# The first three neighbourhood score units, computed in front of the second half of the query projections

## The chip, the cores and the metric

The kernel runs on one core of a Trainium2 chip. The metric is device time in microseconds (us) for one execution, 783.11 us as the median of three runs (781.49 to 783.5). The core has five engines, each with an instruction list of its own: TensorE (PE) multiplies matrices and writes PSUM, VectorE (DVE), ScalarE (ACT) and GpSimd (POOL) work on tiles in SBUF and (the first two) in PSUM, and SyncE (SP) issues the loads. They wait for one another by semaphores.

## The reference, cut to what matters

Two transformer blocks over 256 tokens with 1024 features. The change lies in the attention of the first, which has two mixers side by side: a latent attention (MLA, 8 heads) and a neighbourhood attention (8 heads of 64), whose outputs are joined. Of the second, per head, for the 256 queries in 4 rows of 64 columns:

```
s     = einsum('bqhd,bjkhd->bhqjk', qr, kr) * scale + bias       # own window: all 4 rows, 16 columns near the query
s     = where(col_in, s, MASK_VALUE).reshape(B, H, GRID_W, kh * GRID_W)
s_ctx = einsum('bqhd,bchd->bhqc', qr, k_ctx) * scale             # 256 tokens of context
p     = softmax(concatenate([s, s_ctx], axis=-1))
out   = p_win @ vr + p_ctx @ v_ctx
```

The queries are `hx @ w_in[:, 384:896]`, where `hx` is the normalized and modulated input. After the attention come an output projection, a mixture of 16 experts, and the second block.

## The kernel before, in words

Everything is one function, `build`, which writes out each engine's work. PE's list is kept as written (`MANUAL`); the lists of DVE, ACT and SP are made by a scheduler from the same program, by its own estimate of when things are ready. PE runs float32 in parts: a tile is split into a high part (a cast on ACT, L314) and a low part (a subtraction on DVE, L315), and three matmuls (L334 to L336) multiply high by high, low by high and high by low.

Projections stage. `proj` (eight steps of three matmuls) makes 128 columns at a time. The neighbourhood queries have 512 columns: two weight loads (`c` is 0 or 1), each of two tiles (`j`) of two heads. For each head the result is copied twice, scaled, into both halves of `NQH` (ACT, L647), and the low parts go to `NQL` (DVE, L648); these copies and subtractions of one head take turns. So `c = 0` makes heads 0 to 3, `c = 1` heads 4 to 7. Between them, and after, stand matmuls of the modulation (`mod_step`, L396).

Attention stage. A unit is one block of 128 queries of one head (`Unit`): head 0, 1, 2, ... of the first block, then of the second. `scores` multiplies `NQH` and `NQL` by the head's 512 keys into one PSUM bank (L683, L684), adds the bias in two pieces (DVE, L690) and calls `softmax`: the maximum (DVE, L664), the exponential and its sum (ACT, L667), the reciprocal (DVE, L668), the scaling (DVE, L669). `turn` transposes the result (L698, copied by ACT, L700), and `values` multiplies two units by the values (L710). `attend` runs `scores` three units (`LEAD`) ahead of `turn`, and puts other work, the `fills`, between: first the MLA queries (`uq`: two products, each with weights of its own in two pieces of 768 and 384 columns, tile `qHL`), then the MLA keys and values. `P` is the ring of four buffers that hold the softmax results, `big` a pool of 13 larger tiles, `bank()` a ring of 8 PSUM banks. SP loads weights into a ring of four `raw` buffers, each load waiting until the buffer is free.

Of the kernel before, what the change touches and what calls it, by code (L numbers as in the profile page):

```python
# [10 lines left out]
F32 = mybir.dt.float32  # L11
F32R = mybir.dt.float32r
I32 = mybir.dt.int32
AF = mybir.ActivationFunctionType
OP = mybir.AluOpType
AX = mybir.AxisListType
PSUM = bass.MemoryType.PSUM

P = 128
D = 1024  # L20
KD = 8
T = 256
# [79 lines left out]
LEAD = 3  # L102
# [109 lines left out]
def build(tc, xT, cT, consts, constsA, constsZ, vec, wmod, wA, relb, wE, wC, sgw, sgb, sgln, gfin, out, dbg=None):  # L212
    nc = tc.nc
    vat = VEC_AT
    cat, catA, catZ = [c.at for c in _consts()]
    mm = nc.tensor.matmul
# [6 lines left out]
    with ExitStack() as top:  # L223
# [31 lines left out]
        def vv(name):  # L255
            a, b = vat[name]
            return V[:, a:b]

        def cst(name):
            a, b = cat[name]  # L260
            return C[:, a:b]

        ident = cst("ident")
        cnt = [0]

        def nm_(base):
            cnt[0] += 1
            return f"{base}{cnt[0]}"

        def bank():  # L270
            return psp.tile([P, 512], F32, name=nm_("b"), tag="b")
# [4 lines left out]
        after = [None]  # L276
# [14 lines left out]
        def load(src, n=2048, pl=None, cuts=1):  # L291
            t = (pl or rawp).tile([P, 2048], F32, name=nm_("raw"), tag="raw")
            for a, b in pieces(n, cuts):
                queue(nc.sync.dma_start(t[:, a:b], src[:, a:b]))
            return t

        splitpools = [wp]
        turn = [0]

        def split(src, n=2048, pl=None):  # L300
            return halves(load(src, n, pl), n)
# [27 lines left out]
        def pairhl(name):  # L329
            return (ho.tile([P, KD, T], F32R, name=name + "H", tag="tH"), ho.tile([P, KD, T], F32R, name=name + "L", tag="tL"))  # L330
# [34 lines left out]
        with ExitStack() as sa:  # L365
# [3 lines left out]
            def bigt(shape, name, dt=F32):  # L369
                n = int(np.prod(shape[1:]))  # L370
                t = big.tile([P, 2048], dt, name=name, tag="raw")
                t = t[:shape[0], :n]
                if len(shape) == 3:
                    return t.rearrange("p (a b) -> p a b", a=shape[1])
                if len(shape) == 4:
                    return t.rearrange("p (a b c) -> p a b c", a=shape[1], b=shape[2])
                return t
# [20 lines left out]
            def mod_step(i):  # L398
                due.append((i, load(wmod[8 + i])))
                while len(due) > 1:  # L400
                    mod_mm(*due.pop(0))
# [8 lines left out]
            def mod_cols(hf, rows):  # L410
                pt = bank()
                for i in range(4):
# [3 lines left out]
                nc.vector.tensor_add(mod2[:, o:o + 16].rearrange("p (j i) -> p j i", i=4), src,  # L416
                                     vv("b_mod")[:, 16 + o:32 + o].rearrange("p (j i) -> p j i", i=4))

            oH, oL = pairhl("o")
            with ExitStack() as sp:  # L420
                pp = pool(sp, "pp")
# [129 lines left out]
                class Latent:  # L551
                    def __init__(self, m, n, g, dim, tag, H, L):
                        self.m, self.n, self.g, self.dim, self.tag, self.H, self.L = m, n, g, dim, tag, H, L
                        self.lat = pp.tile([P, m, n], F32, name=f"lat{tag}", tag={"kv": "latkv", "q": "rows3"}[tag])
                        self.sl = pp.tile([P, n], F32, name=f"sl{tag}", tag={"kv": "slkv", "q": "slq"}[tag])
# [18 lines left out]
                NQH = bigt([P, 8, T], "NQH", F32R)  # L574
                NK = [bigt([P, 4, 512], f"NK{i}", F32R) for i in range(2)]
                NQL = bigt([P, 8, T], "NQL", F32R)
# [9 lines left out]
                for c, g in enumerate("BC"):  # L586
                    for j, (hl, ps) in enumerate(early[g]):
                        for hh in range(2):
                            h = 2 * (2 * c + j) + hh
                            own, other = slice(64 * hh, 64 * hh + 64), slice(64 - 64 * hh, 128 - 64 * hh)  # L590
                            k_ = NK[h // 4][:, h % 4]
# [11 lines left out]
                ps = proj(ch[1], 0, 512, 64)  # L603
# [9 lines left out]
                bias = []  # L613
                for i, bt in enumerate((bigt([P, 2048], "bias"), bigt([P, 1024], "biasL"))):
                    n = (32, 16)[i]
# [8 lines left out]
                for c in range(4):  # L624
# [5 lines left out]
                    h, l = ch[c % 2]  # L630
                    for kk in range(2):
                        k = 2 * c + kk
                        s = slice(kk * 512, (kk + 1) * 512)
                        for b in range(4):
                            tb = slice(b * P, (b + 1) * P)
                            mm3(pv[b], (hH[k][:, tb], hL[k][:, tb]), (h[:, s], l[:, s]), k == 0, k == KD - 1)
                for b in range(4):
                    nc.scalar.copy(NV[:, b], pv[b])
                for c in range(2):
                    for j, hl in enumerate(split(wA[5 + c])):  # L640
                        ps = proj(hl, 0, T)
                        for hh in range(2):
                            rw = slice(64 * hh, 64 * hh + 64)
                            other = slice(64 - 64 * hh, 128 - 64 * hh)
                            h = 2 * (2 * c + j) + hh
                            for to in (rw, other):
                                nc.scalar.activation(NQH[to, h], ps[rw, :T], AF.Copy, scale=0.125)  # L647
                                nc.vector.scalar_tensor_tensor(NQL[to, h], ps[rw, :T], 0.125, NQH[rw, h], op0=OP.mult, op1=OP.subtract)  # L648
                    mod_step(5 + c)
                    for i in range(7, NA_FROM if c else 7):  # L650
                        mod_step(i)

            ar = pool(sa, "ar", bufs=2)
            KM = [bigt([96, 4, 512], f"KM{i}") for i in range(2)]
            VM = bigt([P, 4, 512], "VM")
            QM = bigt([96, 8, T], "QM")
            for km in KM:
                nc.vector.tensor_copy(km[64:96], kr[0:32].unsqueeze(1).to_broadcast([32, 4, 512]))

            lexp = [None]  # L660

            def softmax(ps, n):
                nm = ar.tile([P, 1], F32, name=nm_("nm"), tag="nm", bufs=3)
                nc.vector.tensor_reduce(nm, ps, axis=AX.X, op=OP.max, negate=True)  # L664
                rs = ar.tile([P, 1], F32, name=nm_("rs"), tag="rs", bufs=3)
                pt = ar.tile([P, 512], F32, name=nm_("P"), tag="P", bufs=LEAD + 1)
                lexp[0] = nc.scalar.activation(pt[:, :n], ps, AF.Exp, bias=nm, accum_out=rs)  # L667
                nc.vector.reciprocal(rs, rs)  # L668
                after[0] = nc.vector.tensor_scalar(pt[:, :n], pt[:, :n], rs, None, op0=OP.mult)  # L669
                return pt  # L670

            class Unit:
                def __init__(self, pair, na, b, hh, group):
                    self.pair, self.na, self.b, self.hh, self.group = pair, na, b, hh, group

                def scores(self):
                    pair, b, hh = self.pair, self.b, self.hh
                    h = 2 * pair + hh
                    tb = slice(b * P, (b + 1) * P)
                    ps = bank()  # L680
                    if self.na:
                        k_ = NK[h // 4][:, h % 4]
                        mm(ps, NQH[:, h, tb], k_, start=True, stop=False)  # L683
                        mm(ps, NQL[:, h, tb], k_, start=False, stop=True)  # L684
                        pw = ps[:, :T].rearrange("p (r c) -> p r c", r=4)
                        if b:
                            nc.vector.tensor_add(pw, pw, bias[0][:, :, h])
                        else:
                            for i in range(2):
                                nc.vector.tensor_add(pw[:, 2 * i:2 * i + 2], pw[:, 2 * i:2 * i + 2], bias[i][:, 2 - 2 * i:4 - 2 * i, h])  # L690
                    else:
                        mm(ps, QM[:, h, tb], KM[h // 4][:, h % 4], start=True, stop=True)
                    self.p = softmax(ps, 512)

                def turn(self):
                    pt = bank()
                    for kb in range(4):
                        nc.tensor.transpose(pt[:, kb * P:(kb + 1) * P], self.p[:, kb * P:(kb + 1) * P], ident)  # L698
                    self.pS = ar.tile([P, 512], F32, name=nm_("pS"), tag="pS", bufs=4)
                    nc.scalar.copy(self.pS, pt)  # L700

            def values(ua, ub):
                pair, b, na = ua.pair, ua.b, ua.na
                tb = slice(b * P, (b + 1) * P)
# [8 lines left out]
                nc.vector.tensor_sub(oL[:, c, tb], po[:, :P], oH[:, c, tb])  # L713

            def attend(na, fills, every, extra):
                us = [Unit(pair, na, b, hh, None) for b in range(2) for pair in range(4) for hh in range(2)]
                fills = list(fills)
                n = len(us)
                done = 0
                for i in range(LEAD):  # L720
                    us[i].scores()
                for i, u in enumerate(us):
                    if i + LEAD < n:
                        us[i + LEAD].scores()
                    want = -(-len(fills) * (i + 1) // n)
                    while done < want:
                        fills[done]()
                        done += 1
                    u.turn()
                    if i == n - 1:  # L730
                        extra()
                    if i % 2 == 0 and i:
                        values(us[i - 2], us[i - 1])
                    if every:
                        every(i)
                values(us[n - 2], us[n - 1])
# [190 lines left out]
        with sb:  # L927
# [184 lines left out]
            for p in range(8):  # L1112
# [38 lines left out]
                for hf in range(2):  # L1151
                    o = slice(hf * 256, hf * 256 + 256)
                    pt = bank()[:, :256]
# [43 lines left out]
            pw = bank()  # L1197
# [22 lines left out]
        with ExitStack() as sc:  # L1220
# [201 lines left out]
            for c in range(2):  # L1422
                for j, hl in enumerate(csplit(2 + c)):
                    ps = proj2(hl)
# [75 lines left out]
            pw = tokproj(4, {k: F(steps, k) for k in range(KD)})  # L1500
# [152 lines left out]
```

## Time and profile before

| | |
|---|---|
| median of the runs | 783.11 us (781.49 to 783.5) |
| the profiled execution | 783.37 us, of which the span of its instructions 781.7 us |
| PE busy | 97% of the span |
| DVE, ACT, POOL busy | 58%, 46%, 4% |
| mean DMA rate | 254 GB/s |
| mean granted clock of PE | 0.994 of full speed |

All times in the rows below are from the start of the span. A busy share is that of an engine which has an instruction under way; PE's matmuls overlap, so its share tells where it stood still rather than how fast it was. What an engine waited for is read from the idle time before a row. The projections of the queries lie at 110 to 125 us, the neighbourhood attention at 125 to 175 us.

### The profile page before, as it was taken

Reading aid. Unit: us, or ns where it says so; the run is one execution under the profiler, and the core shown is the slowest. Engines: PE = TensorE matmul, PEld = TensorE weight load, DVE = VectorE, ACT = ScalarE, POOL = GpSimd, SP = SyncE. Lnnn points to the kernel's source line nnn. Section 1 sums busy time; section 2 is a strip of 40 time slices with the busy share of each in tenths; the row PEclk is TensorE's granted clock in tenths of the full one; section 3 lists DMA queues with packets and bytes.
Section 4 is the critical chain, followed back from the end, with each engine's and each line's share of the span. In section 5 each row is a group of like instructions: output and inputs, shape, how many; then the busy total and the mean of one; then the engine's idle time right before and its main releaser. Section 6 shows DMA issues by size and latency. Waiting matters only on the chain. (4 is left out here: it accounts for less than half of the span.)

```text
span 781.7 us, 12585 instructions
## 1 busy us (share of the span) xinstructions
PE 761.0 (97%) x5036; PEld 562.5 (72%) x5036; DVE 452.0 (58%) x926; ACT 359.1 (46%) x669; POOL 28.2 (4%) x35
## 2 busy tenths in 40 slices
PE   8999998999999999999999999999999999999996
PEld 7678776766789445535535535898899999999995
DVE  3737639865763123313313336887786877777785
ACT  5527345765663211111102106578766655655654
POOL 0001000000001000000000004103000000000000
PEclk9999999999999999999999999999999999999999
DMA  8867646657959899999999927654443555545301
GB/s 355 339 241 151 254 151 240 232 192 270 419 178 353 346 413 421 419 420 420 420 419 419 415 105 270 231 171 153 135 156 134 200 180 213 199 166 212 109 1 54
DMA packets 29343, 198.86 MB, mean 254 GB/s; under 512 B 3457, under 2 KB 3857, under 8 KB 6369
## 3 DMA queue, kind: packets, MB, share of 16 engines
q1 hardware_dynamic: 28224, 194.45, 64.5%
q0 software_dynamic: 1056, 3.56, 2.0%
q8 instruction: 41, 0.67, 0.4%
q14 instruction: 22, 0.17, 0.1%
HBM read 196.94 MB, written 1.06 MB: 253 GB/s over the span
## 5 line engine op out<-in xcount | busy, mean ns | idle before, releaser
L315 DVE TENSOR_TENSOR w<-raw,w 128x1024 fp32r<-128x1024 f32 (+1 forms) x118 | 140.0, 1213 | 31.3 <-ACT w L314 31.0
L314 ACT CAST w<-raw 128x1024 fp32r<-128x1024 f32 (+1 forms) x118 | 116.5, 1029 | 25.0 <-PE b L336 20.8
L1122 PE MATMUL b<-raw,mix 128*64 128x512 f32 x256 | 113.4, 594 | 0.5 <-issue 0.5
L1121 PE MATMUL b<-raw,mix 128*64 128x512 f32 x256 | 113.4, 594 | 0.3 <-PEq L1070 0.3
L334 PE MATMUL b<-fH,w 128*128 128x256 f32 x352 | 98.7, 280 | 0.0
L336 PE MATMUL b<-fH,w 128*128 128x256 f32 x352 | 98.3, 279 | 0.0
L335 PE MATMUL b<-fL,w 128*128 128x256 f32 x352 | 98.3, 279 | 0.0
L1121 PEld LDWEIGHTS b<-raw,mix 128*64 128x64 f32 x256 | 34.1, 137 | 67.0 <-issue 64.9
L334 PEld LDWEIGHTS b<-fH,w 128*128 128x128 f32 x352 | 66.1, 188 | 0.9
L335 PEld LDWEIGHTS b<-fL,w 128*128 128x128 f32 x352 | 65.9, 187 | 0.9
L336 PEld LDWEIGHTS b<-fH,w 128*128 128x128 f32 x352 | 66.1, 188 | 0.0
L1167 PE MATMUL b<-raw,mix 128*64 128x512 f32 x128 | 56.6, 595 | 0.0
L1168 PE MATMUL b<-raw,mix 128*64 128x512 f32 x128 | 56.6, 595 | 0.0
L1576 ACT ACTIVATE a<-t,V 128x256 f32<-128x256 f32 x44 | 26.3, 599 | 39.0 <-DVE t L1575 38.9
L1167 PEld LDWEIGHTS b<-raw,mix 128*64 128x64 f32 x128 | 16.9, 137 | 33.1 <-issue 32.0
L1156 ACT COPY mix<-b 128x256 f32<-128x256 f32 x16 | 5.4, 374 | 73.5 <-PE b L1155 73.3
L1122 PEld LDWEIGHTS b<-raw,mix 128*64 128x64 f32 x256 | 34.2, 137 | 2.8 <-issue 2.8
L1150 DVE SCALAR_TENSOR_TENSOR mix<-mix,wt,b 128x256 f32<-128x256 f32 x16 | 7.0, 477 | 48.4 <-PE b L1122 43.2
L336 PE MATMUL b<-w,mL 128*128 128x512 f32 x88 | 34.7, 395 | 0.0
L335 PE MATMUL b<-w,mH 128*128 128x512 f32 x88 | 34.7, 394 | 0.0
L334 PE MATMUL b<-w,mH 128*128 128x512 f32 x88 | 34.7, 394 | 0.0
L1172 DVE TENSOR_TENSOR YY<-b,YY 128x512 fp32r<-128x512 f32 x16 | 10.9, 689 | 38.9 <-ACT YY L1172 38.3
(429 smaller groups left out, 1702.5 us busy)
## 6 DMA issues: line engine op xcount, KB each, us to landing
raw<-in_wE SPq DMA_DIRECT2D x94, 1024.0 KB, 14.0
raw<-in_wC SPq DMA_DIRECT2D x46, 1024.0 KB, 4.9
raw<-in_wmod SPq DMA_DIRECT2D x24, 1024.0 KB, 6.8
raw<-in_wA SPq DMA_DIRECT2D x13, 1024.0 KB, 5.0
raw<-in_wE SPq DMA_DIRECT2D x4, 512.0 KB, 17.7
raw<-in_wA SPq DMA_DIRECT2D x2, 576.0 KB, 4.7
X<-in_xT SPq DMA_DIRECT2D x1, 1024.0 KB, 5.2
CX<-in_cT SPq DMA_DIRECT2D x1, 1024.0 KB, 7.4
```

Source lines behind the costliest of these rows:

```text
L314: hc = nc.scalar.copy(h[:, : b - a], raw[:, a:b])
L315: after[0] = (on or nc.vector).tensor_sub(l[:, : b - a], raw[:, a:b], h[:, : b - a])
L334: mm(ps, ah, bh, start=start, stop=False)
L335: mm(ps, ah, bl, start=False, stop=False)
L336: mm(ps, al, bh, start=False, stop=stop)
L1121: la = mm(ps[0:64], XE[:, k, 0:64], wa[:, s], start=k == 0, stop=k == KD - 1)
L1122: lb = mm(ps[64:128], XE[:, k, 64:128], wb[:, s], start=k == 0, stop=k == KD - 1)
L1150: nc.vector.scalar_tensor_tensor(sg[:, o], sg[:, o], wt, pu[:, o], op0=OP.mult, op1=OP.mult)
L1167: la = mm(pd[n][0:64], hd[:, f, 0:64], wa[:, s], start=f == 0, stop=f == 3)
L1168: lb = mm(pd[n][64:128], hd[:, f, 64:128], wb[:, s], start=f == 0, stop=f == 3)
L1172: ylast = (nc.scalar.copy(yH[:, o], pd[n]), nc.vector.tensor_sub(yL[:, o], pd[n], yH[:, o]))
L1576: nc.scalar.activation(a, t, AF.Identity, bias=bcv[:, n:n + 1], scale=wcv[:, 2, n:n + 1])
```

## The change

`scores` and `softmax` are defined earlier in the file, and the units of the neighbourhood attention (`na_units`) are made once. The scores of the first three, heads 0, 1 and 2, are computed between the first half of the query projections (`c = 0`) and the second (`c = 1`). Their results, maxima and sums lie in one tile of the `big` pool, `ahead`, and not in the ring `P`. `attend` then starts the neighbourhood units without its own three.

```diff
+            def softmax(ps, n, at=None):
+                if at is None:
+                    nm = ar.tile([P, 1], F32, name=nm_("nm"), tag="nm", bufs=3)
+                    ...
+                else:
+                    pt, nm, rs = [ahead[0][:, a:b] for a, b in ((512 * at, 512 * at + 512), (1536 + at, 1537 + at), (1540 + at, 1541 + at))]
+                nc.vector.tensor_reduce(nm, ps, axis=AX.X, op=OP.max, negate=True)
+                ...
+            def units(na):
+                return [Unit(pair, na, b, hh, None) for b in range(2) for pair in range(4) for hh in range(2)]
+
+            na_units = units(True)
...
                 for c in range(2):
+                    if c:
+                        ahead.append(bigt([P, 2048], "ahead"))
+                        for i in range(LEAD):
+                            na_units[i].scores(i)
                     for j, hl in enumerate(split(wA[5 + c])):
                         ps = proj(hl, 0, T)
...
             def attend(na, fills, every, extra):
-                us = [Unit(pair, na, b, hh, None) for b in range(2) for pair in range(4) for hh in range(2)]
+                us = na_units if na else units(False)
...
-                for i in range(LEAD):
+                for i in range(0 if na else LEAD):
                     us[i].scores()
```

On PE, behind the first half of the query projections (the last row with `w_927`) and the modulation (L396), before:

```order
L336 MATMUL b_963<-hH_176,w_927 128x256
L396 MATMUL b_685<-raw_864,sil 32x512 x4
L334 MATMUL b_1010<-hH_175,w_1004 128x256
L335 MATMUL b_1010<-hL_177,w_1004 128x256
L336 MATMUL b_1010<-hH_175,w_1004 128x256
```

and now (L447 and L448 are the score matmuls, L683 and L684 of before):

```order
L336 MATMUL b_963<-hH_176,w_927 128x256
L396 MATMUL b_685<-raw_864,sil 32x512 x4
L447 MATMUL b_1003<-NK_566,NQH 128x512
L448 MATMUL b_1003<-NK_566,NQL 128x512
L447 MATMUL b_1012<-NK_566,NQH 128x512
L448 MATMUL b_1012<-NK_566,NQL 128x512
L447 MATMUL b_1021<-NK_566,NQH 128x512
L448 MATMUL b_1021<-NK_566,NQL 128x512
L334 MATMUL b_1038<-hH_175,w_1032 128x256
```

Six matmuls stand in front of the second half; behind it one unit's two are left of four units' eight.

On DVE at the same place, from the low part of the second half's second weight tile on, before (`b_930` and `b_963` are the banks of heads 0 and 1 and of heads 2 and 3, `b_1010` that of heads 4 and 5):

```order
L315 TENSOR_TENSOR w_1007<-raw_1002,w_1007 128x1024
L648 SCALAR_TENSOR_TENSOR NQL<-b_930,NQH 64x256
L648 SCALAR_TENSOR_TENSOR NQL<-b_963,NQH 64x256
L648 SCALAR_TENSOR_TENSOR NQL<-b_930,NQH 64x256
L648 SCALAR_TENSOR_TENSOR NQL<-b_963,NQH 64x256
L648 SCALAR_TENSOR_TENSOR NQL<-b_1010,NQH 64x256
L648 SCALAR_TENSOR_TENSOR NQL<-b_963,NQH 64x256
L658 COPY KM_1093<-kr 32x2048
```

and now (`b_1003`, `b_1012` and `b_1021` are the score banks of the three units, L454 the bias add, `b_1038` the bank of heads 4 and 5):

```order
L315 TENSOR_TENSOR w_1035<-raw_1030,w_1035 128x1024
L454 TENSOR_TENSOR b_1003<-b_1003,bias 128x128
L703 SCALAR_TENSOR_TENSOR NQL<-b_930,NQH 64x256
L703 SCALAR_TENSOR_TENSOR NQL<-b_963,NQH 64x256
L454 TENSOR_TENSOR b_1003<-b_1003,biasL 128x128
L703 SCALAR_TENSOR_TENSOR NQL<-b_930,NQH 64x256
L703 SCALAR_TENSOR_TENSOR NQL<-b_963,NQH 64x256
L454 TENSOR_TENSOR b_1012<-b_1012,bias 128x128
L703 SCALAR_TENSOR_TENSOR NQL<-b_963,NQH 64x256
L454 TENSOR_TENSOR b_1012<-b_1012,biasL 128x128
L454 TENSOR_TENSOR b_1021<-b_1021,bias 128x128
L454 TENSOR_TENSOR b_1021<-b_1021,biasL 128x128
```

Bias adds of the three units now stand between the splits of heads 1 to 3.

On DVE ahead of the second `uq` weights, before (the last two rows are their low parts; `b_1043` is the bank of heads 6 and 7):

```order
L664 TENSOR_REDUCE nm_1104<-b_1099 128x1
L664 TENSOR_REDUCE nm_1116<-b_1111 128x1
L780 TENSOR_TENSOR ta_1230<-b_1155,CA 128x64
L781 TENSOR_TENSOR tb_1231<-b_1155,CA 128x64
L664 TENSOR_REDUCE nm_1128<-b_1123 128x1
L648 SCALAR_TENSOR_TENSOR NQL<-b_1043,NQH 64x256
L315 TENSOR_TENSOR w_1177<-raw_1175,w_1177 128x768
L315 TENSOR_TENSOR w_1180<-raw_1175,w_1180 128x384
```

and now (the last row is the first of them):

```order
L430 RECIPROCAL ahead<-ahead 128x1
L703 SCALAR_TENSOR_TENSOR NQL<-b_1038,NQH 64x256
L703 SCALAR_TENSOR_TENSOR NQL<-b_1071,NQH 64x256
L431 TENSOR_SCALAR ahead<-ahead 128x512 x2
L454 TENSOR_TENSOR b_1127<-b_1127,biasL 128x128
L431 TENSOR_SCALAR ahead<-ahead 128x512
L793 TENSOR_TENSOR ta_1222<-b_1147,CA 128x64
L794 TENSOR_TENSOR tb_1223<-b_1147,CA 128x64
L703 SCALAR_TENSOR_TENSOR NQL<-b_1038,NQH 64x256
L703 SCALAR_TENSOR_TENSOR NQL<-b_1071,NQH 64x256
L428 TENSOR_REDUCE nm_1132<-b_1127 128x1
L315 TENSOR_TENSOR w_1169<-raw_1167,w_1169 128x768
```

The three units' reciprocals and scalings, which stood behind these weights, now stand in front of them; so do the two copies L713 (L658 of before) and the first `uq` weights, a little further up.

## Rows read from the trace of the kernel before

**Rows 1.** The page, busy time (share of the span) and instructions of each engine.

```profile
PE 761.0 (97%) x5036; PEld 562.5 (72%) x5036; DVE 452.0 (58%) x926; ACT 359.1 (46%) x669; POOL 28.2 (4%) x35
```

**Rows 2.** Windows: us, busy of PE, PEld, DVE, ACT, POOL (instructions), PEclk, DMA share, GB/s.

```profile
132.90:134.45 1.55, 0.40 (x1) 0.15 (x2) 1.49 (x4) 1.52 (x5) 0.00 (x0) 0.87 0.25 106
134.45:137.40 2.95, 2.95 (x9) 2.95 (x10) 2.92 (x12) 0.78 (x2) 0.00 (x0) 0.50 0.50 136
137.50:138.90 1.40, 1.40 (x9) 1.37 (x9) 1.33 (x9) 0.00 (x0) 0.00 (x0) 1.00 1.02 433
150.00:170.00 20.00, 20.00 (x164) 14.01 (x165) 13.41 (x39) 14.35 (x35) 0.00 (x0) 1.00 0.49 165
260.00:400.00 140.00, 139.28 (x770) 66.01 (x768) 38.29 (x100) 22.50 (x46) 0.52 (x1) 1.00 1.01 416
```

**Rows 3.** Timeline of PE: start us, us, instruction, [idle before <-releaser]; `uq` to first transposes.

```profile
129.40 0.41 PE L334 MATMUL b<-w,qHL 128*128 128x384 f32 x1 [0.55 <-DVE NQL L648]
...
132.86 0.44 PE L334 MATMUL b<-w,qHL 128*128 128x384 f32 x1 [1.66 <-ACT P L667]
...
134.45 0.69 PE L335 MATMUL b<-w,qHL 128*128 128x384 f32 x1 [1.15 <-DVE w L315]
...
138.90 0.60 PE L698 MATMUL b<-C,P 128*128 128x128 f32 x4
```

**Rows 4.** Timeline of PE: start of the projections' second half, first scores, `uq`.

```profile
117.36 0.38 PE L334 MATMUL b<-hH,w 128*128 128x256 f32 x1
...
125.16 0.50 PE L683 MATMUL b<-NK,NQH 128*128 128x512 f32 x1
125.49 0.40 PE L684 MATMUL b<-NK,NQL 128*128 128x512 f32 x1
...
127.10 0.33 PE L334 MATMUL b<-w,qHL 128*128 128x384 f32 x1
```

**Rows 5.** Timeline of DVE, 119 to 137 us.

```profile
119.07 2.75 DVE L648 SCALAR_TENSOR_TENSOR NQL<-b,NQH 64x256 fp32r<-64x256 f32 x6
121.85 2.35 DVE L658 COPY KM<-kr 32x2048 f32<-32x2048 f32 x2
...
125.66 1.43 DVE L315 TENSOR_TENSOR w<-raw,w 128x768 fp32r<-128x768 f32 x2 [0.56 <-ACT w L314]
...
127.92 0.87 DVE L690 TENSOR_TENSOR b<-b,bias 128x128 f32<-128x128 f32 x4
...
129.28 0.50 DVE L690 TENSOR_TENSOR b<-b,biasL 128x128 f32<-128x128 f32 x2
...
130.80 1.29 DVE L664 TENSOR_REDUCE nm<-b 128x1 f32<-128x512 f32 x2
...
133.44 1.43 DVE L315 TENSOR_TENSOR w<-raw,w 128x768 fp32r<-128x768 f32 x2
...
135.72 0.21 DVE L668 RECIPROCAL rs<-rs 128x1 f32<-128x1 f32 x2
136.10 1.27 DVE L669 TENSOR_SCALAR P<-P,rs 128x512 f32<-128x512 f32 x3
```

**Rows 6.** Timeline of ACT, 119 to 143 us.

```profile
119.53 0.83 ACT L647 ACTIVATE NQH<-b 64x256 fp32r<-64x256 f32 x2 [0.95 <-DVE NQL L648]
120.53 1.23 ACT L647 ACTIVATE NQH<-b 64x256 fp32r<-64x256 f32 x3 [0.17 <-PE b L336]
...
124.80 1.25 ACT L314 CAST w<-raw 128x768 fp32r<-128x768 f32 x2 [1.01 <-DMA raw<-in_wA]
...
139.70 1.99 ACT L314 CAST w<-raw 128x1024 fp32r<-128x1024 f32 x2 [2.31 <-DMA raw<-in_wA]
141.60 1.55 ACT L700 COPY pS<-b 128x512 f32<-128x512 f32 x3
```

**Rows 7.** Timelines of PE and SP: the first values, the issue of the key/value weights.

```profile
142.43 0.83 PE L710 MATMUL b<-pS,NV 128*64 128x128 f32 x8
...
134.89 0.33 SPq L294 DMA_DIRECT2D raw<-in_wA  x1
```

More of the change, by code (lines that the diff above doesn't have):

```diff
@@ L417, in mod_cols @@
                                      vv("b_mod")[:, 16 + o:32 + o].rearrange("p (j i) -> p j i", i=4))
+            lexp = [None]
+            def softmax(ps, n, at=None):
+                if at is None:
+                    nm = ar.tile([P, 1], F32, name=nm_("nm"), tag="nm", bufs=3)
+                    rs = ar.tile([P, 1], F32, name=nm_("rs"), tag="rs", bufs=3)
+                    pt = ar.tile([P, 512], F32, name=nm_("P"), tag="P", bufs=LEAD + 1)
+                else:
+                    pt, nm, rs = [ahead[0][:, a:b] for a, b in ((512 * at, 512 * at + 512), (1536 + at, 1537 + at), (1540 + at, 1541 + at))]
+                nc.vector.tensor_reduce(nm, ps, axis=AX.X, op=OP.max, negate=True)
+                lexp[0] = nc.scalar.activation(pt[:, :n], ps, AF.Exp, bias=nm, accum_out=rs)
+                nc.vector.reciprocal(rs, rs)
+                after[0] = nc.vector.tensor_scalar(pt[:, :n], pt[:, :n], rs, None, op0=OP.mult)
+                return pt
@@ new lines, in build, with __init__, scores, turn @@
+            ahead = []
+            class Unit:
+                def __init__(self, pair, na, b, hh, group):
+                    self.pair, self.na, self.b, self.hh, self.group = pair, na, b, hh, group
+                def scores(self, at=None):
+                    pair, b, hh = self.pair, self.b, self.hh
+                    h = 2 * pair + hh
+                    tb = slice(b * P, (b + 1) * P)
+                    ps = bank()
+                    if self.na:
+                        k_ = NK[h // 4][:, h % 4]
+                        mm(ps, NQH[:, h, tb], k_, start=True, stop=False)
+                        mm(ps, NQL[:, h, tb], k_, start=False, stop=True)
+                        pw = ps[:, :T].rearrange("p (r c) -> p r c", r=4)
+                        if b:
+                            nc.vector.tensor_add(pw, pw, bias[0][:, :, h])
+                        else:
+                            for i in range(2):
+                                nc.vector.tensor_add(pw[:, 2 * i:2 * i + 2], pw[:, 2 * i:2 * i + 2], bias[i][:, 2 - 2 * i:4 - 2 * i, h])
+                    else:
+                        mm(ps, QM[:, h, tb], KM[h // 4][:, h % 4], start=True, stop=True)
+                    self.p = softmax(ps, 512, at)
+                def turn(self):
+                    pt = bank()
+                    for kb in range(4):
+                        nc.tensor.transpose(pt[:, kb * P:(kb + 1) * P], self.p[:, kb * P:(kb + 1) * P], ident)
+                    self.pS = ar.tile([P, 512], F32, name=nm_("pS"), tag="pS", bufs=4)
+                    nc.scalar.copy(self.pS, pt)
@@ L658, in build @@
                 nc.vector.tensor_copy(km[64:96], kr[0:32].unsqueeze(1).to_broadcast([32, 4, 512]))
[L660 to L700, printed above, removed]
             def values(ua, ub):
```

## The prediction

> **What bounds the kernel now.** Begin with the page's busy shares: TensorE (PE) is busy for 97% of the span [rows 1], so the place to look for is where it isn't. The windows table says the same by stage: it has work for all of 150 to 170 us and for 139.28 of the 140 us from 260 to 400 [rows 2]. The timeline of PE around the seam between the projections and the neighbourhood attention shows the hole [rows 3]. In the two products that make the latent queries (`uq`, tile `qHL`) it idles 0.55 us until the query split on VectorE (DVE) lets a bank go, 1.66 us until the first exponential frees another, and 1.15 us until DVE has made the low part of the second weight tile: 3.36 us in all. Inside that stretch the granted clock falls to half: nine matmuls take 2.95 us at 0.50 and 1.40 us at 1.00 [rows 2], 1.55 us more. So 4.9 us at this seam is what a better order could win. DVE has no such holes there: its rows follow each other from 125.66 to 134.87 [rows 5]. The trace has the rows of DVE and ScalarE (ACT) in the order of their lists, so what counts is what stands ahead of each thing PE waits for.
>
> **The change part by part.** The computation is the same. Six score matmuls (three units of two) go in front of the 48 matmuls of the second half of the query projection; with them go six bias adds, three reductions, three exponentials, three reciprocals and three scalings on DVE and ACT. No DMA is added, and SP's list keeps its order; but each load waits for a buffer to come free, so it moves with whatever frees it.
>
> *Step 1, the scores in their new place.* Before, PE starts the second half at 117.36 [rows 4]. Now unit 0 starts there: its two matmuls need head 0 alone, split by then. They are done by about 118.1 (0.33 us to the second, 0.40 us for it). Unit 1 needs head 1, whose last low part is the third of the six splits that DVE starts at 119.07, 0.46 us each (2.75/6), so it ended at 120.45 [rows 5]. In the new list a bias add stands ahead of these splits and another between them [the order of DVE]; at 0.22 to 0.25 us a piece [rows 5], with the changes of kind, the third split ends at about 121.0. ACT's half of the handshake confirms that this can't come early: its next query copy started at 119.53, after waiting 0.95 us for DVE [rows 6]. So PE has nothing to do from 118.1 to about 121.2, but for one matmul: 3.1 us idle. Units 1 and 2 then end, and the second half starts at about 121.9 instead of 117.36: 4.5 us later, 1.4 of them the moved scores (four units took 1.94 us [rows 4]). The 1.4 come back later, where one unit is left of four. This wait is new; behind it on PE stand all 48 projection matmuls, and for those wait ACT's next query copy, DVE's next split, and all that stands behind these two.
>
> *Step 2, DVE runs dry, then late.* The remaining splits and adds are done at about 123.1. Next on its list is the split of the second half's first tile. ACT's copy of that tile started 3.17 us after the projections' start (120.53 against 117.36 [rows 4, 6]), so now at 125.07; DVE, which was never short of work here, idles some 2.3 us. ACT then casts the first `uq` weights: its query copy takes 0.41 us (1.23/3), and the low part followed the cast's start by 0.86 us (125.66 against 124.80) [rows 5, 6]. So DVE starts this low part at 125.07 + 0.41 + 0.86, about 126.3, against 125.66.
>
> *Step 3, from that low part to the one that PE waits for.* Before, DVE needed 8.74 us from 125.66 to the end of the larger low part of the second `uq` weights (the first of the two rows from 133.44; it let PE go at 134.45, so about 134.40). The list between the same two places now has: one split more (+0.46); two bias adds instead of eight (the eight took 0.87 + 2 x 0.50 = 1.87, two take 0.22 + 0.25: -1.40); one reduction more (1.29/2: +0.65); both key copies, which stood in front of this stretch and now stand in it (+2.35); three scalings (+1.27) and three reciprocals (0.21 for two: +0.3), which stood behind it [rows 5]. Sum +3.63: 12.4 us, from 126.3 to 138.7. The durations in runs of equal kind overlap a little more than this allows, so I take 138.6. PE's second matmul of the second `uq` product went at 134.45 [rows 3]; it now goes at about 138.6, 4.2 us later. Inside the stretch there is another wait, for the small low part of the first weights (132.8 against 131.5 when PE comes there), but it lies ahead of the larger one and costs nothing more.
>
> *Step 4, to the first values.* PE reached the first transposes at 138.90 [rows 3], with 2.95 us of the way at half clock. If the clock falls again, the 4.2 us stay; if not, 1.55 of them come back here, and are lost again a little later: the load of the key/value weights is issued when DVE has freed the buffer of the second `uq` weights (134.89, right behind the second small low part), ACT casts it on landing (139.70, after 2.31 us of waiting) and has the copies of the transposed scores behind these casts (141.60) [rows 6, 7]. All of these move by 4.2 us, so PE's first values go at 146.6 and not at 142.43 [rows 7], by either way. What the three finished units spare there (DVE has their scalings behind it, the transposes find them ready) hides behind that.
>
> *Step 5, to the end.* After that PE's list and the others' are as before, and PE has no holes that could take 4 us up: 20.00 of 20 us and 139.28 of 140 [rows 2]. The expert weights run at a DMA share of 1.01 from 260 to 400 [rows 2], but they too are issued as buffers come free, so the stream starts later with the rest. The larger tile that holds the three units takes a free place in its pool; its first writer waits for a matmul of the second half (about 126), before DVE gets there anyway: nothing.
>
> Bounds. A load took 4.8 us to its cast (139.70 - 134.89) [rows 6, 7]; should the key/value weights meet other loads, as much as 1 us more is possible. The sum of step 3 may be 0.3 short or 0.5 long. The clock in step 1 has two ends: unharmed (0), or half for as long as before, at 1.55 us for nine matmuls [rows 2]. I take 0, since the rows show the fall only behind three idle pieces, 3.36 us together, within 5.6 us. The Trainium skill (TensorE: Matmul & The Clock Gate, "HAM oscillation") warns that idle pieces between bursts of matmuls bring the low clock back and that the next burst starts cold; by it the new hole of step 1 would cost a second fall, which is rival B below. No run so far shows a hole of that shape.
>
> The profiled execution took 783.37 us for a span of 781.7; the median of the runs is 783.11, 0.26 less. 783.37 + 4.2 = 787.6 on the profile's own scale, **787.3** on that of the median.
>
> **The rivals.**
> A. The forecast: 787.3, of itself 786.3 to 788.3. Chance 0.62.
> B. The clock falls a second time, behind the scores' wait. The idle time (2.3 us, one matmul, 0.5 us) speaks for it; that the 0.55 us alone in [rows 3] was followed by full speed, and that there are fewer pieces than before, against. The first projection tile, on which step 2 hangs, would come up to 1.55 us later, and all behind it: 788.8. Chance 0.15.
> C. The wait at the scores stands, but the old stalls go for it, as the exponentials now lie earlier: 4.5 - 1.4 = +3.1 at the seam, less 3.36 and 1.55: 781.3. For it: two of the three waits are for a bank that an exponential or a split frees, and these come sooner now. Against it: the third is for DVE, and DVE's list is what I summed. Chance 0.13.
> D. The other side: the scores' wait does not come about, because head 1 is split when PE gets there, and all 4.9 us of the old seam go: 778.2. It is decided at one place, DVE's third split of the six: it would have to end by 118.1, and it ended at 120.45 [rows 5]. The change doing just what its place suggests has this one row against it. Chance 0.07.
> E. As A, but some 2 us are taken up before the end, at the loads that PE waits for: 785.3. Chance 0.03.
>
> **How the numbers follow.** 0.3% is 2.35 us, about what a measurement of this kernel can tell: faster is under 780.8, slower over 785.5. A and B are slower but for a rest of A (0.02): 0.75. C, E and that rest: 0.18. D, rounded down for nothing: 0.07. The range leaves out C and D, 0.2 together: from 784.0, into E's side, to 789.2, B with half a microsecond for the load's bound.
>
> **What would show it.** Step 1: a PE row of the scores' fourth matmul with an idle time released by DVE's `NQL`, and the second half's first projection near 121.9. Step 2: DVE idle some 2 us before a split, released by ACT's `NQH`. Step 3: PE's `qHL` row released by DVE `w`, near 138.6. Step 4: the first values near 146.6, behind ACT's casts. Step 5: all later rows shifted by the same amount. A projection start before 119, or a low part of the second `uq` weights before 136, would make the prediction wrong; a granted clock of 0.50 near 121 would be B.

## The result and the profile after

The changed kernel takes 787.97 us (median of 6 runs) against 782.44 for the kernel before on the same chip: ratio 1.0079, 95% interval 1.0068 to 1.0091, slower by 5.5 us of median (the medians by themselves give 1.0071). The profiled execution has a span of 788.0 us and is the longest of the six, at 789.65 us. Its page gives the shares that answer to [rows 1]; PE's and DVE's busy times hardly tell where the time went.

```profile
PE 765.0 (97%) x5036; PEld 565.6 (72%) x5036; DVE 452.3 (57%) x926; ACT 359.0 (46%) x669; POOL 28.2 (4%) x35
```

The windows of the changed kernel, with the columns of [rows 2]:

```profile
20.00:40.00 20.00, 18.19 (x106) 11.49 (x105) 13.99 (x26) 9.41 (x15) 0.00 (x0) 0.91 0.81 310
123.28:126.26 2.98, 2.98 (x15) 2.98 (x14) 1.13 (x4) 0.00 (x0) 0.00 (x0) 0.50 0.51 196
126.50:130.40 3.90, 3.90 (x34) 3.83 (x32) 1.99 (x4) 1.48 (x3) 0.00 (x0) 1.00 0.00 0
140.90:146.50 5.60, 5.54 (x17) 5.51 (x18) 3.23 (x14) 0.00 (x0) 0.00 (x0) 0.50 0.52 190
```

The first row lies 80 us ahead of the change, and I take it to have nothing to do with it: this execution lost some clock at 20 to 40 us (0.91), and so everything at the seam stands 1.46 us later than in the other trace even before it begins (the modulation step ahead of it starts at 117.82, against 116.36 before). I take 1.46 off when I compare times. The other rows do belong to the change: a half clock (0.50, the lower of the two levels) at the start of the second half, where before there was none, and a longer one in the second `uq` product.

The timeline of PE, answering to [rows 3, 4]:

```profile
118.81 0.50 PE L447 MATMUL b<-NK,NQH 128*128 128x512 f32 x1
...
121.63 0.50 PE L447 MATMUL b<-NK,NQH 128*128 128x512 f32 x1 [2.08 <-ACT NQH L702]
122.33 0.50 PE L448 MATMUL b<-NK,NQL 128*128 128x512 f32 x1 [0.20 <-DVE NQL L703]
...
123.28 0.41 PE L334 MATMUL b<-hH,w 128*128 128x256 f32 x1
...
135.26 0.44 PE L335 MATMUL b<-w,qHL 128*128 128x384 f32 x1 [0.99 <-DVE w L315]
...
138.00 0.44 PE L334 MATMUL b<-w,qHL 128*128 128x384 f32 x1 [0.54 <-ACT w L314]
140.96 0.69 PE L335 MATMUL b<-w,qHL 128*128 128x384 f32 x1 [2.51 <-DVE w L315]
...
146.56 0.72 PE L462 MATMUL b<-C,ahead 128*128 128x128 f32 x4
...
150.22 1.09 PE L723 MATMUL b<-pS,NV 128*64 128x128 f32 x16
```

Unit 0 goes at once; unit 1 waits 2.08 us for ACT's copies and 0.20 for DVE's split of head 1. Behind it a projection matmul takes 0.41 us and not 0.28. The last wait, 2.51 us, is for the low part of the second `uq` weights; no matmul of the tile behind it waits again, but all run at half clock. The lists of DVE, ACT and SP (rows 5 to 7 of before):

```profile
124.18 0.30 DVE L454 TENSOR_TENSOR b<-b,biasL 128x128 f32<-128x128 f32 x1
128.10 0.42 DVE L703 SCALAR_TENSOR_TENSOR NQL<-b,NQH 64x256 fp32r<-64x256 f32 x1 [3.62 <-ACT NQH L702]
128.83 0.96 DVE L315 TENSOR_TENSOR w<-raw,w 128x768 fp32r<-128x768 f32 x1 [0.31 <-ACT w L314]
129.70 1.88 DVE L428 TENSOR_REDUCE ahead<-b 128x1 f32<-128x512 f32 x3
131.61 1.22 DVE L713 COPY KM<-kr 32x2048 f32<-32x2048 f32 x1
...
139.94 0.96 DVE L315 TENSOR_TENSOR w<-raw,w 128x768 fp32r<-128x768 f32 x1
...
127.69 0.38 ACT L702 ACTIVATE NQH<-b 64x256 fp32r<-64x256 f32 x1 [4.55 <-PE b L336]
...
146.56 2.00 ACT L314 CAST w<-raw 128x1024 fp32r<-128x1024 f32 x2 [5.83 <-DMA raw<-in_wA]
148.46 0.58 ACT L464 COPY pS<-b 128x512 f32<-128x512 f32 x1
...
141.53 0.33 SPq L294 DMA_DIRECT2D raw<-in_wA  x1
```

DVE stands still for 3.62 us behind the last bias add, since ACT waits 4.55 us for PE's first tile of the second half. From the first `uq` low part (128.83) DVE is busy without a gap to the second (139.94), and SP's load of the key/value weights is issued behind it, at 141.53.

### The profile page after: what moved, and what is told of

Same layout as the page of the kernel before. It is cut to its first block, busy times and chain, and to the rows that moved or that the text cites. A ratio compares the mean times of both kernels' runs of the same rounds, so it can differ in the third digit from the quotient of the medians.

```text
span 788.0 us, 12579 instructions
## 1 busy us (share of the span) xinstructions
PE 765.0 (97%) x5036; PEld 565.6 (72%) x5036; DVE 452.3 (57%) x926; ACT 359.0 (46%) x669; POOL 28.2 (4%) x35
```

## The experiments

All are in ratio to the kernel before, run on the same chip in the same rounds. Where two experiments are compared, it is by what each has over the kernel before of its own rounds; for the changed kernel that is 5.5 us. Traces are compared by the time from the modulation step ahead of the seam. Each kernel has one trace. The theory: PE's new wait for head 1 makes ACT and DVE run dry, and DVE's longer list carries the delay to the second `uq` weights and, through the load behind them, to the first values. The rivals say that one of these links costs nothing, or that the tile `ahead` costs by itself.

### One unit in front

```diff
-                        for i in range(LEAD):
+                        for i in range(1):
                             na_units[i].scores(i)
...
-                for i in range(0 if na else LEAD):
-                    us[i].scores()
+                for i in range(1 if na else 0, LEAD):
+                    us[i].scores(i if na else None)
```

> Only unit 0 (head 0) is computed in front of the second half; units 1 and 2 go back behind it, their results still in the tile `ahead`. Theory W (the wait of PE for head 1's split starts the loss, and what stands in DVE's list behind it carries it on): no wait is left in front of the second half, which starts one unit, 0.7 us, later than before at most; DVE's list from the first to the second `uq` weights sums to 9.0 us against 8.74 before; so 782 to 784 us, within 0.2% of before. Rival T (the tile `ahead` and the unit computed early cost by themselves, whatever waits): 786 or more.

783.29 us, ratio 1.0009 (1.0000 to 1.0019). Its PE has no wait in front of the second half, and one at the second `uq` product:

```profile
134.31 0.44 PE L335 MATMUL b<-w,qHL 128*128 128x384 f32 x1 [3.22 <-DVE w L315]
```

134.31 stands against 134.45 before, though the seam of this execution begins 0.4 us sooner (its modulation step at 115.97). So the tile and the early place of one unit cost some 1.1 us by the medians (782.15 was the kernel before in these rounds), at most 1.5 by the interval; the rest is what two more units bring.

### The three units behind the second half

```diff
                 for c in range(2):
-                    if c:
-                        ahead.append(...); three units
                     for j, hl in enumerate(split(wA[5 + c])):
                         ...
+                    if c:
+                        ahead.append(...); three units
                     mod_step(5 + c)
```

> The three units stand behind the second half, in front of its modulation step, results in `ahead`. No head is waited for there. If the wait alone makes the loss: 782.5 us, as before. If DVE's list also makes a part of its own (both key copies, 2.35 us, one scaling and one reciprocal now between the first and the second `uq` weights: 10.3 us against 8.74): 1.6 us over before, 784. Rival T (tile and place cost by themselves): 786 or more.

784.06 us, ratio 1.0024 (1.0013 to 1.0035): the wait at the scores is gone, and with it 3.6 us of the changed kernel's 5.5; some 1.9 us stay against the 782.15 of before in these rounds. DVE's list of this kernel shows why:

```profile
125.67 0.96 DVE L315 TENSOR_TENSOR w<-raw,w 128x768 fp32r<-128x768 f32 x1
126.55 0.68 DVE L428 TENSOR_REDUCE ahead<-b 128x1 f32<-128x512 f32 x1
127.26 2.35 DVE L713 COPY KM<-kr 32x2048 f32<-32x2048 f32 x2
...
134.66 0.95 DVE L315 TENSOR_TENSOR w<-raw,w 128x768 fp32r<-128x768 f32 x1
```

The first low part starts when it did before (125.66), the second ends at 135.61 instead of about 134.4: softmax work and both copies stand between. Behind it the second `uq` product took 5.60 us, all at half clock, against 4.45 before.

### Unit 0, 1 and 2 spread over the second half

```diff
+                        na_units[0].scores(0)          # in front of c = 1
...
                         ps = proj(hl, 0, T)
+                        if c:
+                            na_units[1 + j].scores(1 + j)
```

> The changed kernel, with unit 0 in front of the second half, unit 1 behind its first tile and unit 2 behind its second, so that PE has 24 projection matmuls to do while head 1 and head 2 are split. All three softmaxes still lie early, in `ahead`. DVE's list from the first to the second `uq` weights sums to 7.7 us against 8.74 before and 12.4 in the changed kernel, with two reductions and both copies in front of it. If it is the wait that makes the early scores dear: no wait there, 781 to 783 us. If early softmaxes delay DVE wherever the scores stand: 784 to 786.

784.2 us, ratio 1.0019 (1.0009 to 1.0028), 2.2 us over the kernel before: by the median, the second of the two expectations. The trace does not bear it out. PE has no wait at the scores, and the sum between the two low parts is as short as expected; but the reductions, copies and adds stand in front of the first of them, which starts 128.92 - 1.35 = 127.57 and not at 125.66 (this execution too stands 1.35 us late at the seam). That delay is all but made up by the second, the one that PE waits for:

```profile
124.64 1.29 DVE L428 TENSOR_REDUCE ahead<-b 128x1 f32<-128x512 f32 x2
125.96 1.22 DVE L714 COPY KM<-kr 32x2048 f32<-32x2048 f32 x1
127.21 0.43 DVE L704 SCALAR_TENSOR_TENSOR NQL<-b,NQH 64x256 fp32r<-64x256 f32 x1
127.67 1.22 DVE L714 COPY KM<-kr 32x2048 f32<-32x2048 f32 x1
128.92 0.96 DVE L315 TENSOR_TENSOR w<-raw,w 128x768 fp32r<-128x768 f32 x1
...
135.03 0.94 DVE L315 TENSOR_TENSOR w<-raw,w 128x768 fp32r<-128x768 f32 x1
...
136.03 0.44 PE L335 MATMUL b<-w,qHL 128*128 128x384 f32 x1 [1.78 <-DVE w L315]
```

It ends at 134.62 on the scale of before (135.97 - 1.35), against 134.40. The first values come 0.9 us later than before, and in the experiment with the units behind the second half 2.8 us later. So without PE's wait three early softmaxes cost the seam 0.9 to 2.8 us, by where they fall in DVE's list, and not the changed kernel's 6.3. Where the rest of this run's 2.2 us of median lies its trace does not show.

### The key copies on POOL, in the changed kernel and before

```diff
-                nc.vector.tensor_copy(km[64:96], kr[0:32]...)
+                nc.gpsimd.tensor_copy(km[64:96], kr[0:32]...)
```

> The changed kernel, but the two key copies (2.35 us) are made by POOL and not by DVE. If DVE's list sum sets when PE gets the second `uq` weights, as step 3 has it: 2.4 us less than the changed kernel, 785.6 us, and the wait of PE for that low part 2.4 us shorter. If only PE's wait at the scores matters, or ACT's part of the chain: 788, no change. The wait at the scores and the half clock behind it stay in both.

785.58 us, ratio 1.0054 (1.0037 to 1.0071): 3.4 us over the kernel before, where the changed kernel is 5.5 over it. This is near the 2.4 us expected, but the list gives only a part of it:

```profile
127.28 0.96 DVE L315 TENSOR_TENSOR w<-raw,w 128x768 fp32r<-128x768 f32 x1 [0.31 <-ACT w L314]
...
136.84 0.96 DVE L315 TENSOR_TENSOR w<-raw,w 128x768 fp32r<-128x768 f32 x1
...
137.85 0.44 PE L335 MATMUL b<-w,qHL 128*128 128x384 f32 x1 [1.57 <-DVE w L315]
...
142.49 0.60 PE L462 MATMUL b<-C,ahead 128*128 128x128 f32 x4
```

From the first low part's start to the second's end it is 10.52 us, against 12.07 in the changed kernel: 1.55 less and not 2.35, since another low part took 0.84 us longer beside POOL's copies (the rows are in the last section). PE goes on 1.55 us sooner. The other 0.96 us is the clock: the product behind the wait takes 4.64 us to the transposes and not 5.60.

> The kernel before with the two key copies on POOL. There they stand in a piece of DVE's list that ends in 0.56 us of waiting for the first `uq` weights. If the copies cost only where they stand between the first and the second `uq` weights (as in the changed kernel, where taking them away gave 2.4 us): no change, 781.8 to 782.6. If they cost wherever they stand: 780.

782.65 us, ratio 1.0003 (0.9990 to 1.0016): nothing. Taking the same two copies off DVE gains 2.1 us where they stand ahead of the awaited low part and nothing where they fill a hole.

### PE's wait filled

```diff
+                        for _ in range(filler):                      # 9 for unit 1, else 0
+                            mm(ps, NQH[:, 0, tb], NK[0][:, 0], start=True, stop=True)
                         mm(ps, NQH[:, h, tb], k_, start=True, stop=False)
```

> The changed kernel with nine extra score matmuls in PE's wait for head 1, in front of unit 1's own and overwritten by them (some 2.1 us, as long as the idle time). If the half clock at the start of the second half costs of its own: the granted clock stays at 1.00 there, the first `uq` weights' low part comes 1.2 us earlier and all behind it, 786.7 us. If the clock's loss is hidden by DVE's list: 788 as the changed kernel. If the extra matmuls outlast the wait: up to 0.3 us on top.

787.63 us, ratio 1.0063 (1.0049 to 1.0077): inconclusive in the median, clear in the trace of PE:

```profile
117.77 2.24 PE L448 MATMUL b<-NK,NQH 128*128 128x512 f32 x9
...
121.53 0.28 PE L334 MATMUL b<-hH,w 128*128 128x256 f32 x1
...
137.87 0.69 PE L335 MATMUL b<-w,qHL 128*128 128x384 f32 x1 [2.50 <-DVE w L315]
...
142.49 0.60 PE L464 MATMUL b<-C,ahead 128*128 128x128 f32 x4
...
457.95 0.61 PE L1136 MATMUL b<-raw,mix 128*64 128x512 f32 x1 [2.09 <-PEq L1085]
```

The second half runs at 0.28 us a matmul, full clock. From the modulation step ahead (116.21 here) to the wait at 137.87 it is 21.66 us, against 23.14 in the changed kernel: 1.5 us gained, as expected. The product behind that wait, which is as long as in the changed kernel (2.50 and 2.51 us), took 4.62 us to the transposes and not 5.60, so that these come 2.5 us sooner; how long the half clock lasts is thus not set by the wait in front of it alone. The last row takes it back: at the end of the experts PE waited 2.09 us for its own sequencer, where it was 0.31 in the other traces, and ran at a clock of 0.74 from 460 to 464 us behind that. Two of the six runs took 786.1 and 786.3 us, four 787.6 to 788.1. Why that late wait grew stays open.

### A modulation step in the wait

```diff
                         for i in range(LEAD):
                             na_units[i].scores(i)
+                            if i == 0:
+                                mod_step(5)
```

> The changed kernel with one modulation step (1.06 us) moved from in front of unit 0 to between unit 0 and unit 1: no instruction added, PE idles 1.1 us and not 2.1 for head 1. Head 1's split comes when ACT and DVE are through, wherever PE is, so the second half starts no earlier than in the changed kernel: 788 if only the wait's end counts and the clock falls behind it as before; 786.5 if the clock then stays at 1.00 in the second half (1.3 to 1.5 us, as the filled wait showed at this seam); 785.5 if PE's idle time counted by itself.

787.34 us, ratio 1.0060 (1.0046 to 1.0074), not told apart from the changed kernel (1.0068 to 1.0091). PE still idled 1.82 us, and the clock fell as before:

```profile
121.21 0.50 PE L447 MATMUL b<-NK,NQH 128*128 128x512 f32 x1 [1.82 <-ACT NQH L704]
...
122.52 0.41 PE L334 MATMUL b<-hH,w 128*128 128x256 f32 x1
```

The expectation of 1.1 us of idle time was wrong by its own terms: the step came from in front of unit 0, so PE reaches unit 1 with the same work behind it as in the changed kernel, and head 1's copies set the end of the wait. So this run says nothing of work added to the wait; it shows the fall of the clock a second time.

### The larger piece of the second `uq` weights in a tile of its own

```diff
-                ws_ = halves(load(wA[10 + g], 1152), 1152, step=768)
+                ws_ = halves(load(wA[10 + g], 1152), 1152, step=768, first=big if g else None)
```

> The changed kernel, but the larger piece of the second `uq` weights has a tile of its own in the pool `big`, so that its split need not wait for PE to be done with the first `uq` weights; it then stands some 4 us earlier in DVE's list. The wait at the scores and the half clock behind it stay. If this low part is what carries the delay on (step 3): PE's wait of 2.5 us for it goes, and with it the half clock of the second product, 783 to 784.5 us. If the load of the key/value weights carries it (step 4; it waits for the smaller piece, which moves by 1.3 us only): 786.5 us.

786.0 us, ratio 1.0039 (1.0027 to 1.0052): 3.2 us over the kernel before (782.77 in these rounds) instead of 5.5, between the two numbers expected. The trace says that both are right, one behind the other. PE's rows, and ACT's:

```profile
142.22 0.60 PE L464 MATMUL b<-C,ahead 128*128 128x128 f32 x4
...
147.48 1.09 PE L725 MATMUL b<-pS,NV 128*64 128x128 f32 x14 [1.30 <-ACT pS L466]
...
144.96 1.99 ACT L316 CAST w<-raw 128x1024 fp32r<-128x1024 f32 x2 [1.51 <-DMA raw<-in_wA]
146.85 1.07 ACT L466 COPY pS<-b 128x512 f32<-128x512 f32 x2
```

The first transposes come 4.1 us sooner than in the changed kernel (142.22 against 146.56; unit 0 starts at 118.59 here, 0.22 us sooner), and the product in front of them runs at full clock. But the values then wait 1.30 us for the copies that stand behind the casts of the key/value weights, whose load had to wait for the smaller piece. That is the second half of step 4, shown by itself.

### The same, on the kernel before and with one unit

```diff
-                ws_ = halves(load(wA[10 + g], 1152), 1152, step=768)
+                ws_ = halves(load(wA[10 + g], 1152), 1152, step=768, slots=big if g else None)
```

> The kernel before, but both pieces of the second `uq` weights have tiles in `big`. DVE then makes them in front of the three reductions. If PE's third wait there (1.15 us, for the low part) is a cost by itself: it goes, with the half clock behind it, 779.5 to 781 us. If it only changes places: the reductions and so the first exponential come 1.4 us later, PE's wait for the bank that this frees grows from 1.66 to 3.1 us, and the time stays at 782.

781.75 us, ratio 0.9993 (0.9980 to 1.0006): not told apart from before. In its trace the wait for the low part is gone, the one for the exponential's bank did not grow, and the transposes start at 136.05 instead of 138.90, in an execution that stands 0.45 us sooner at the seam:

```profile
132.77 0.44 PE L334 MATMUL b<-whl,qHL 128*128 128x384 f32 x1 [1.74 <-ACT P L667]
...
136.05 0.63 PE L698 MATMUL b<-C,P 128*128 128x128 f32 x4
```

The median keeps less than half of these 2.4 us (781.75 against 782.77); the runs spread from 780.95 to 785.35, and the profiled one is the shortest.

> One unit in front of the second half (as in the first experiment), and the larger piece of the second `uq` weights in a tile of `big`. The early unit's exponential frees its bank long before the second `uq` product, and the low part stands in front of the other reductions. If the seam's holes are DVE's list and bank alone: PE's wait of 3.2 us goes, with the half clock behind it (1.5 us); the load of the key/value weights comes 2.3 us earlier; 777.5 to 780 us, faster than both. If the load or the copies of the transposed scores set the first values anyway: 781 to 782.

Unit 0 in front, and the larger piece alone in `big`: 782.72 us, ratio 0.9991 (0.9977 to 1.0005). The lower number did not come. In the profiled execution the values waited 2.83 us for ACT's copies, behind casts that waited for the load:

```profile
144.82 1.09 PE L725 MATMUL b<-pS,NV 128*64 128x128 f32 x14 [2.83 <-ACT pS L466]
```

That execution is the longest of the twelve (784.88; the shortest took 779.88), and in it the load took 7.5 us from its issue at 134.79 to the cast at 142.30, against 4.8 before. Whether the others waited as long is not shown.

### All limits together

```diff
-                        ahead.append(bigt([P, 2048], "ahead"))
-                        for i in range(LEAD):
+                        ahead.append(spare[0])       # the unused half of the tile biasL
+                        for i in range(1):
...
+                ws_ = halves(load(wA[10 + g], 1152), 1152, step=768, slots=big if g else None)
```

> Unit 0 alone in front of the second half, its result in the unused half of the tile `biasL`; both pieces of the second `uq` weights in tiles of `big`, so that the `raw` buffer comes free, and the key/value weights are loaded, some 3.5 us earlier (issued at 131.3 and not at 134.9, as in the kernel before with both pieces in `big`). If the three limits named so far are all there is (the bank that unit 0's exponential frees, the low part, the load): PE's waits at the seam shrink from 3.4 us to about 1, the half clock behind them goes, 778 to 780 us. If the other splits and banks then stop PE for as long: 781.5, as the kernel before with the weights in `big`.

780.59 us, ratio 0.9984 (0.9971 to 0.9997): faster than both kernels, though only by 1.5 us than the one before; with the next the only ones whose interval lies below 1. In the profiled execution, the shortest of the twelve at 778.91, a wait of 1.87 us for a query split and one of 0.28 among the first values are left at the seam; the load is issued at 131.46, against 134.89 [rows 7]:

```profile
132.03 0.41 PE L334 MATMUL b<-whl,qHL 128*128 128x384 f32 x1 [1.87 <-DVE NQL L706]
```

> As the last, and the two key copies on POOL. If they still stand in a hole of DVE's list: the same time as the last, within 0.5 us. If the first `uq` weights' low part has become later than its load: up to 1 us less.

781.38 us, ratio 0.9989 (0.9980 to 0.9998): no gain on the last one. DVE's list came out in another order, so this run does not say what the copies cost there: the low part of the second `uq` weights starts at 132.15 and not at 129.80, and PE waits for it:

```profile
133.15 0.45 PE L335 MATMUL b<-whl,qHL 128*128 128x384 f32 x1 [2.64 <-DVE whl L315]
```

## Why the prediction was right, and which terms were off

787.3 was forecast, 787.97 measured, slower, inside the range. Step by step, the trace's times less 1.46:

| step | before | forecast | measured |
|---|---|---|---|
| 1: second half starts | 117.36 | 121.9 | 121.82 |
| 2: ACT copies its first tile | 120.53 | 125.07 | 126.23 |
| 2: first `uq` low part | 125.66 | 126.3 | 127.37 |
| 3: PE goes on with the second `uq` weights | 134.45 | 138.6 | 139.50 |
| 4: first transposes | 138.90 | up to 143.1 | 145.10 |
| 4: first values | 142.43 | 146.6 | 148.76 |

*Step 1* came as told: the wait for head 1, 4.46 us of shift. Its releaser was ACT's copy for 2.08 us and DVE's split, which the prediction named, for 0.20. What failed in it is the clock, which I took at nothing: from the second half's start to ACT's first copy it took 4.41 us (127.69 - 123.28) against 3.17. So the term "I take 0" measured 1.24 us; rival B had 1.55 for it. The filled wait, in which the clock stayed up and 1.5 us came back at the seam, shows that the hole made it: in the three other traces with this hole unfilled (the copies on POOL, the larger piece in `big`, the modulation step) the clock fell behind it too. The length of a hole does not tell by itself: behind the 1.74, 1.87 and 2.83 us shown above, the clock stayed at 1.00.

*Step 2* held: DVE idle 3.62 us behind its last add, which is the 2.3 forecast and the clock's part.

*Step 3* held, and is the best supported: 12.07 us from the first low part's start to the second's end (140.90 - 128.83) against 12.3 forecast and 8.74 before. With the copies on POOL it was 1.55 us shorter, and PE went on 1.55 us sooner; doing the low part earlier took 4.1 us off the way to the transposes.

*Step 4* had the right mechanism and the wrong size. I let the half clock in the second product last as long as before, or go; it lasted for the whole product, 5.60 us from its wait to the transposes (146.56 - 140.96) against 4.45, 1.15 us more. The load did come late: ACT's first copy of the transposed scores, behind the casts, started at 148.46 and took 0.58 us, so that the values could not have gone before 147.6 on the scale of the table, and the experiment with the larger piece shows them waiting for such copies. Here the half clock was later still. So the seam lost 6.3 us and not 4.2: 1.24 and 1.15 for the clock, 0.2 less for the list.

*Step 5* held but for one place. In the stage ahead of the experts the same eight matmuls took (before, then now):

```profile
247.75 3.05 PE L976 MATMUL b<-mix,ones 128*128 128x256 f32 x8
...
254.72 1.89 PE L989 MATMUL b<-mix,ones 128*128 128x256 f32 x8
```

The clock was 0.56 from 247 to 250.5 us before, and 1.00 from 251 to 258.4 now, and this stage (from 243.87 to 251.85, and from 251.35 to 258.31) is 1.0 us shorter. All three traces of kernels without early units have the longer form, all eleven with them the shorter; with one trace of each kernel, whether this goes with the change or with the execution stays open. The 1.46 us are a fall that five of the fourteen traces show.

So the nearness of the number is in part luck. The seam lost 2.1 us more than forecast; by the end of the experts 1.3 of the 6.3 had come back (460.18 - 117.82 is 5.0 us more than 453.72 - 116.36), which no step had. And the forecast was added to 783.11, while the kernel before had a median of 782.44 when the two were compared: 5.5 us between the medians, where 4.2 were forecast.

Rival B, at 0.15, is what happened in its mechanism, by the sign that was named for it: the clock of 0.50 begins at 121.82 on the scale of the table. Its 788.8 is about as far above the measurement as the forecast is below. The Trainium skill (TensorE: Matmul & The Clock Gate, "HAM oscillation") describes such a fall behind waits of some 3 to 5 us between bursts of matmuls. Here a wait of 2.08 us was enough, as the rows at 0.50 show. Rival D fell by the row on which it hung, DVE's third split. Rival C fell by the old stalls, which changed their releasers and grew: 0.99, 0.54 and 2.51 us, 4.04 in all against 3.36.

## What to carry to other kernels

Before moving work forward on one engine, find the last input it needs and what stands ahead of that on the other engines' lists; unit 0 was ready, units 1 and 2 were not, and one unit cost a fifth of what three did. Then sum the other engine's list up to the next thing that is waited for: what is moved forward of it is paid for (12.07 us in place of 8.74), what falls into a hole is free. A hole on PE can also cost behind itself, when the clock falls.

## What the runs showed of the hardware

Two key copies take 2.35 us on DVE and 4.14 on POOL (3.72 in the kernel before), and while POOL made them a DVE low part of 384 columns took 1.38 us and not 0.54. Row of POOL, and of DVE, in the changed kernel with the copies on POOL:

```profile
127.68 4.14 POOL L713 COPY KM<-kr 32x2048 f32<-32x2048 f32 x2 [64.18 <-PE b L336]
...
130.85 1.38 DVE L315 TENSOR_TENSOR w<-raw,w 128x384 fp32r<-128x384 f32 x1
```

So 2.35 us taken off DVE's list made it 1.55 us shorter. It stayed a gain, since DVE was the one that PE waited for.
